# Reading a bias table back in four parts through another DMA queue, and a reworked attention stage: one core of a Trainium2 chip

## The chip, the core and the metric

One Trainium2 chip, one of its cores. The metric is the time of one execution of the program in microseconds (us). TensorE (PE) multiplies matrices and transposes, VectorE (DVE) and ScalarE (ACT) work on elements, GpSimd (POOL) does small things, and SyncE (SP) issues most of the DMAs. Each engine runs its instructions in the order in which the program hands them over; what orders the engines among themselves are semaphores.

## What is computed

A trunk of two layers on 256 tokens of width 1024, in float32. Layer 0 mixes with a state-space mixer (S5); layer 1 with sparse attention whose keys and values are computed once, between the layers.

```python
for layer in range(DEPTH):
    h = h + 0.5 * _swiglu(_rmsnorm(h, ffn1_norm[layer]), ffn1_w_in[layer], ffn1_w_out[layer])
    u = _rmsnorm(h, mix_norm[layer])
    if layer < N_A_LAYERS:
        h = h + _s5_mixer(u, ...)
    else:
        h = h + _nsa_mixer(u, kv, w_qg[b], q_norm[b], w_o[b], rel_bias)
    h = h + 0.5 * _swiglu(_rmsnorm(h, ffn2_norm[layer]), ffn2_w_in[layer], ffn2_w_out[layer])
    if layer == N_A_LAYERS - 1:
        kv = _shared_kv(h, ...)
```

In the attention, the queries of 16 heads of 64 (4 heads share one of 4 key groups) are normalised per head. Each head has three branches (compressed, selected and window keys), each a softmax over query times key plus a bias that depends on the distance of the two positions, `rel_bias[_rel_bucket(dist)]`. A gate per head and branch, the sigmoid of further columns of the query product, weighs the branches; the sum goes through `w_o`. With 256 tokens all causal blocks are selected and the window holds all tokens, so selected and window keys are both 128 columns for the first 128 tokens and 256 for the second.

## The kernel before

**Matmuls.** Tokens stand in two tiles of 128, t = 0 and 1. Every float32 product is made of three products of rounded parts (`mm3`, L126 to L128): the activations' rounding (hi) times the weights' hi, hi times the weights' remainder (lo), and lo times hi. So each weight is split on chip after loading: a granule of 1 MB lands in one of two `raw` buffers (`load_granule`, SP's queue), ACT rounds it (`whi`; L92 plain, L105 times a norm's gain), and DVE makes the remainder (`wlo`; L96, L108). There are five buffers of each. `Acts` holds a stage's transposed activations: `turn` transposes (PE), `place` writes their hi (ACT) and lo (DVE), `fill` does both for four column groups of a tile.

**Stages, in order.** First FFN of layer 0, to about 205 us; the S5 mixer to about 268; second FFN of layer 0 to about 460; the shared keys and values to about 505; first FFN of layer 1 to 700.5; attention to 808.5; second FFN of layer 1 to the end. Outside S5 and attention a scheduler at build time sets each engine's order, from the order of the program and its own estimates of when data arrives.

**An FFN** runs over 11 chunks of 256 hidden columns. A chunk takes eight `w_in` slices, 48 matmuls of 512 columns into two PSUM banks `mm`. ACT and DVE make the gated activation g (L306, L307). PE transposes the g of the chunk before (L265) in the middle of the products, ACT and DVE copy it out (`turned`, L151, L152), and 24 matmuls with `w_out` add to the result.

**The bias table.** While the second FFN of layer 0 runs, the generator `bias_tables` is stepped in its gaps (`background`, one step per two of a chunk's eight slices, paced by what each `yield` returns). It makes one row `rev` of biases per head, writes it to DRAM scratch `revd` (two DMAs), and reads it back as `KV.B`, 128 rows by 16 heads by 256 distances, each row shifted by one against the next, in eight DMAs of 256 KB on SP's queue (L846). SP's queue also carries the granules. `B` is read first in the attention.

**Attention** is an order written by hand: `ORDER` is a string of steps, and each step is issued on its engines in that order, which the scheduler keeps for PE, ACT and DVE. The letters that matter here: d, h, w load and split a part of the query weights; f, F, J fill the activations of tile 1; Q, R its norm; g the query product, four parts per group n and tile t into one `mm` bank; a to x the normalisation of its heads and the transposes (a squares and copies out of the bank on ACT, b the mean on DVE and the power -1/2 on POOL, n multiplies, i and j split, y transposes, x copies out); l the logits of one head into a bank `s` (and `x` for t = 1); v adds bias and takes the maximum (DVE), e the exponential and its sum (ACT), s and S scale the probabilities by 1/sum and gate (DVE); t transposes them and T copies them to SBUF; c, k, q, z, C, K, Z are the compressed branch; P is the product with the values, o and O copy it out; D, H, W load and split `w_o`, and M is the product with it; the last letters prepare the next FFN.

PSUM has two banks each of `mm`, `tr` (transposes), `s` and `x`. A bank is handed out again in turn, and the first matmul into it waits until all readers of its last contents are done.

## Time and profile before

| | |
|---|---|
| median of three runs | 998.76 us (998.57 to 1000.18) |
| the profiled execution, in all | 1000.22 us |
| its span, first to last instruction | 998.5 us |
| granted TensorE clock, mean over the span | 1.00 |
| PE busy | 969.4 us, 97% |
| DVE, ACT, POOL busy | 659.0, 577.1, 80.6 us |

Every row below comes from the one profiled execution. The engine that is nearly full is PE; what a stage can lose or give back is where PE waits. PE's busy time overlaps from one matmul to the next, so waits also show as fewer matmuls in a stretch of equal length.

### The profile page before, as it was taken

The numbers are of one execution on the slowest core, as the hardware profiler recorded it, in microseconds if no ns is written. First come the engines' busy times: TensorE is split into PE (matmuls) and PEld (weight loads), VectorE is DVE, ScalarE is ACT, GpSimd is POOL, SyncE is SP. The second block draws the span as 40 slices with busy tenths as digits, with TensorE's granted clock in tenths as the row PEclk, the third lists the DMA queues.
The fourth block names the chain that finished last, engine by engine and source line by source line (L and its number), as shares of the span: only waits on it lengthen the run. The fifth ranks groups of instructions, "written<-read, shape, count | busy, mean of one in ns | idle before, by whom it ended". The sixth has DMA issues, their size and how long they took to land.

```text
span 998.5 us, 14337 instructions
## 1 busy us (share of the span) xinstructions
PE 969.4 (97%) x5523; PEld 794.1 (80%) x5523; DVE 659.0 (66%) x1210; ACT 577.1 (58%) x1023; POOL 80.6 (8%) x91
## 2 busy tenths in 40 slices
PE   6999999999999989999999999999988999999998
PEld 5788788788878867788878888888876778888886
DVE  4998875579964544657566556565899676555553
ACT  5677666463663543656656545454888565555552
POOL 3001012312200000000032000000200000000000
PEclk9999999999999999999999999999999999999999
DMA  7555565433357556564644445554431235555551
GB/s 270 192 192 202 174 208 177 164 94 146 97 190 212 158 174 216 185 228 151 248 169 166 170 171 197 182 189 135 127 107 43 85 127 211 193 186 185 195 179 74
DMA packets 28948, 168.96 MB, mean 169 GB/s; under 512 B 4560, under 2 KB 7184, under 8 KB 10064
## 3 DMA queue, kind: packets, MB, share of 16 engines
q1 hardware_dynamic: 28656, 167.26, 49.7%
q8 instruction: 43, 0.70, 0.3%
q0 software_dynamic: 224, 0.79, 0.2%
q14 instruction: 25, 0.20, 0.1%
HBM read 165.54 MB, written 2.49 MB: 168 GB/s over the span
## 4 chain that ended last, share of the span: by engine, by line
PE 78%; DVE 11%; ACT 5%; DMA 4%; issue 1%; POOL 1%; SPq 0%; ACTq 0%
PE mm L126 15%; PE mm L127 15%; PE mm L128 14%; PE o L128 7%; PE o L127 7%; PE o L126 7%; DMA raw<-in_w_in_dram 3%; DVE wlo L96 3%; PE tr L265 2%; ACT whi L92 1%; DVE Pt L1153 1%; PE dr L596 1%; PE tr L945 1%; PE ga L126 1%; PE ga L128 1%
## 5 line engine op out<-in xcount | busy, mean ns | idle before, releaser
L126 PE MATMUL mm<-whi,xT 128*128 128x512 f32 (+2 forms) x800 | 312.4, 392 | 6.1 <-ACT whi L92 2.6
L127 PE MATMUL mm<-wlo,xT 128*128 128x512 f32 (+2 forms) x800 | 306.3, 383 | 0.7 <-DVE wlo L96 0.5
L128 PE MATMUL mm<-whi,xT 128*128 128x512 f32 (+2 forms) x800 | 305.9, 383 | 0.0
L108 DVE SCALAR_TENSOR_TENSOR wlo<-raw,gains,whi 128x512 fp32r<-128x512 f32 x274 | 192.7, 748 | 86.7 <-ACT whi L105 84.1
L105 ACT ACTIVATE whi<-raw,gains 128x512 fp32r<-128x512 f32 x274 | 182.6, 718 | 98.8 <-PE mm L128 50.1
L96 DVE TENSOR_TENSOR wlo<-raw,whi 128x1024 fp32r<-128x1024 f32 x132 | 160.5, 1224 | 104.4 <-ACT whi L92 103.8
L92 ACT ACTIVATE whi<-raw 128x1024 fp32r<-128x1024 f32 x132 | 138.4, 1059 | 121.5 <-PE mm L128 51.5
L126 PEld LDWEIGHTS mm<-whi,xT 128*128 128x128 f32 x800 | 150.7, 189 | 37.1 <-ACT whi L105 3.1
L127 PEld LDWEIGHTS mm<-wlo,xT 128*128 128x128 f32 x800 | 151.1, 189 | 29.4 <-DVE wlo L96 1.5
L128 PEld LDWEIGHTS mm<-whi,xT 128*128 128x128 f32 x800 | 150.7, 188 | 29.3
L128 PE MATMUL o<-whi,turned 128*128 128x512 f32 x352 | 137.5, 391 | 0.8 <-DVE turned L152 0.8
L127 PE MATMUL o<-wlo,turned 128*128 128x512 f32 x352 | 137.6, 391 | 0.1
L126 PE MATMUL o<-whi,turned 128*128 128x512 f32 x352 | 136.8, 391 | 0.0
L128 PEld LDWEIGHTS o<-whi,turned 128*128 128x128 f32 x352 | 66.1, 188 | 15.0 <-DVE turned L152 1.5
L127 PEld LDWEIGHTS o<-wlo,turned 128*128 128x128 f32 x352 | 66.1, 188 | 14.4 <-DVE wlo L96 1.0
L126 PEld LDWEIGHTS o<-whi,turned 128*128 128x128 f32 x352 | 66.0, 188 | 13.7
L306 ACT ACTIVATE g<-mm,rs 128x256 f32<-128x256 f32 x88 | 41.0, 472 | 45.2 <-PE mm L128 44.9
L307 DVE SCALAR_TENSOR_TENSOR g<-mm,rs,g 128x256 f32<-128x256 f32 x88 | 41.7, 482 | 36.2 <-ACT g L306 36.1
L152 DVE TENSOR_TENSOR turned<-tr,turned 128x512 fp32r<-128x512 f32 x44 | 30.3, 688 | 36.1 <-ACT turned L151 35.7
L151 ACT ACTIVATE turned<-tr 128x512 fp32r<-128x512 f32 x44 | 26.1, 593 | 45.9 <-PE tr L265 45.9
L148 POOL TENSOR_TENSOR rs<-ms,nhalf 128x1 f32<-128x1 f32 x12 | 7.6, 633 | 284.4 <-DVE ms L147 284.4
L1160 ACT ACTIVATE Pt<-Pt,mx 128x128 f32<-128x128 f32 (+1 forms) x64 | 28.3, 446 | 3.7 <-DVE mx L1153 3.7
(321 smaller groups left out, 982.0 us busy)
## 6 DMA issues: line engine op xcount, KB each, us to landing
raw<-in_w_in_dram SPq DMA_DIRECT2D x87, 1024.0 KB, 4.9
raw<-in_w_out_dram SPq DMA_DIRECT2D x44, 1024.0 KB, 4.9
raw<-in_w_kv_dram SPq DMA_DIRECT2D x6, 1024.0 KB, 4.8
raw<-in_w_glu_dram SPq DMA_DIRECT2D x4, 1024.0 KB, 4.9
raw<-in_w_o_dram SPq DMA_DIRECT2D x4, 1024.0 KB, 5.0
raw<-in_w_qg_dram SPq DMA_DIRECT2D x6, 512.0 KB, 3.6
B<-revd SPq DMA_DIRECT2D x8, 256.0 KB, 7.5
raw<-in_w_qg_dram SPq DMA_DIRECT2D x2, 608.0 KB, 3.8
```

The source lines that it names most:

```text
L92: Last.act = S.activation(hi, r, AF.Copy)
L96: Last.dve = V.tensor_tensor(out=lo, in0=r, in1=hi.bitcast(F32), op=ALU.subtract)
L105: Last.act = S.activation(hi[:, c], r[:, c], AF.Identity, scale=g_)
L108: i = V.scalar_tensor_tensor(out=lo[:, c], in0=r[:, c], scalar=g_, in1=hi[:, c].bitcast(F32), op0=ALU.mult, op1=ALU.subtract)
L126: T.matmul(ps, lhsT=xh, rhs=wh, start=start, stop=False)
L127: T.matmul(ps, lhsT=xh, rhs=wl, start=False, stop=False)
L128: Last.pe = T.matmul(ps, lhsT=xl, rhs=wh, start=False, stop=stop_)
L151: i = S.activation(dst_hi, src, AF.Copy)
L152: V.tensor_tensor(out=dst_lo, in0=src, in1=dst_hi.bitcast(F32), op=ALU.subtract)
L306: Last.act = S.activation(sl, acc[t][:, 0:256], AF.Silu, scale=rs[:, t:t + 1])
L307: Last.dve = V.scalar_tensor_tensor(out=g[:, t, :], in0=acc[t][:, 256:512], scalar=rs[:, t:t + 1], in1=sl, op0=ALU.mult, op1=ALU.mult)
L1160: S.activation(p_, p_, AF.Exp, scale=-1.0, bias=mx[g, t][:, c:c + 1], accum_out=sm[g, t][:, c:c + 1])
```

## The change

**Bias table.** The host lays `rel_bias` out so that 32 rows of `rev` hold four heads, eight times. `revd` becomes four scratch tensors of four heads. For each of them two DMAs on SP's queue write it from 32 rows of `rev`, and eight DMAs on GpSimd's queue, of 64 KB, read it back into `B` (L845 after): 32 reads in place of 8, of the same bytes in all. Every read is followed by a `yield` of one step.

**Fill with a gain** (`Acts.fill`): the roundings of all four column groups (ACT) are issued ahead of the four remainders (DVE), where the two alternated.

**Attention.** Step a only squares, unscaled; the scaled copy `qs` is gone (eight ACT instructions, L1094), step n reads the bank itself, and step b takes the row's mean in place of a constant so that the missing scale cancels. The gate's tanh is a step of its own (p). Key columns of tile 0's logits stand in another order, so that one matmul of 272 columns takes what 400 took (32 matmuls, L1138). The multiplication by `vcol` is done once in G in place of once per group in k. Step s is the reciprocal alone, and S multiplies by both the reciprocal and the gate (64 instructions, L1205). Of the 24 copies of transposed probabilities, 21 (T) are on ACT and 3 (X) on DVE, where each had 12. `ORDER` is a new list, of 399 steps for 397. The diff shows one line of it, before and after; new names of the same lines and some unchanged lines are left out.

```diff
@@ -142,8 +142,8 @@
...
-    def row_rstd(t, ss, rs):
-        ms = small.tile([P, 1], F32, name="ms")
+    def row_rstd(t, ss, rs, ms=None):
+        ms = small.tile([P, 1], F32, name="ms") if ms is None else ms[:, t:t + 1]
         V.scalar_tensor_tensor(out=ms, in0=ss[:, 2 * t:2 * t + 1], scalar=EPS, in1=ss[:, 2 * t + 1:2 * t + 2], op0=ALU.add, op1=ALU.add)
         G.tensor_tensor(out=rs[:, t:t + 1], in0=ms, in1=nhalf[:, 0:1], op=ALU.pow)
@@ -159,6 +159,7 @@
...
+            self.ms = small.tile([P, 2], F32, name="mean")
@@ -192,8 +193,7 @@
...
             else:
-                for j in range(4):
-                    i = [self.place(u, t, kq, pv, (j,)) for u in range(2)][0]
+                i = [self.place(u, t, kq, pv) for u in range(2)][0]
@@ -835,16 +835,15 @@
...
         yield
-        dr = dscr.tile([16, 16, 384], F32, name="revd")
-        for r in range(2):
-            nc.sync.dma_start(out=dr[8 * r:8 * r + 8].rearrange("q h k -> (q h) k"), in_=rev)
-            yield
-        yield
         KV.B = kp.tile([P, 16, 256], F32, name="B")
-        for r in range(8):
-            src = bass.AP(tensor=dr.tensor, offset=dr.offset + 127 - 16 * r, ap=[[16 * 384 - 1, 16], [384, 16], [1, 256]])
-            nc.sync.dma_start(out=KV.B[16 * r:16 * r + 16], in_=src)
-            yield 4
+        for n in range(4):
+            dr = dscr.tile([16, 4, 384], F32, name=f"revd{n}")
+            for q in range(2):
+                nc.sync.dma_start(out=dr[8 * q:8 * q + 8].rearrange("q h k -> (q h) k"), in_=rev[32 * n:32 * n + 32])
+            for r in range(8):
+                src = bass.AP(tensor=dr.tensor, offset=dr.offset + 127 - 16 * r, ap=[[4 * 384 - 1, 16], [384, 4], [1, 256]])
+                nc.gpsimd.dma_start(out=KV.B[16 * r:16 * r + 16, 4 * n:4 * n + 4], in_=src)
+                yield
@@ -934,7 +933,7 @@
...
-                    c0 = (n - 1) * KWN + t * P
+                    c0 = (1 - t) * P if n == 1 else KWN + t * P
@@ -995,21 +994,21 @@
...
-    Q0 f0 d10 g000 F00 f1 g001 J00 d11 F01 h100 F10 J01 w100 d20 F11 g010 J10 g002 h110 J11 Q1 g011 g003 g012 R g013 a00 w110 b00
...
+    d10 g000 Q0 d11 h100 f0 w100 g001 f1 g002 F00 F01 d20 J01 g003 F11 J00 Q1 J11 g010 g011 a00 R F10 b00 J10 h110 p0 g012 w110
...
@@ -1074,7 +1073,7 @@
...
             def step_R():
-                row_rstd(1, x.ss, rs)
+                row_rstd(1, x.ss, rs, x.ms)
@@ -1086,30 +1085,28 @@
...
             def step_a(n, t):
-                q, v = tp.tile([P, 256], F32, name="qs"), tp.tile([P, 4, 2, 64], F32R, name="qst")
-                qq[n, t], qv[n, t] = q, v
-                if n == 0:
-                    S.activation(rsh[:, t:t + 1], rs[:, t:t + 1], AF.Copy, scale=0.5)
-                S.activation(v.rearrange("p h a d -> p (h a d)")[:, 0:256].bitcast(F32), qa[n, t][:, 0:256], AF.Square, scale=rs[:, t:t + 1])
-                S.activation(q, qa[n, t][:, 0:256], AF.Identity, scale=rs[:, t:t + 1])
-                if n == 0:
-                    S.activation(gate[:, t].rearrange("p h b -> p (h b)"), qa[n, t][:, 256:304], AF.Tanh, scale=rsh[:, t:t + 1])
+                qq[n, t], qv[n, t] = tp.tile([P, 256], F32, name="qs"), tp.tile([P, 4, 2, 64], F32R, name="qst")
+                S.activation(qv[n, t].rearrange("p h a d -> p (h a d)")[:, 0:256].bitcast(F32), qa[n, t][:, 0:256], AF.Square)
+
+            def step_p(t):
+                S.activation(rsh[:, t:t + 1], rs[:, t:t + 1], AF.Copy, scale=0.5)
+                S.activation(gate[:, t].rearrange("p h b -> p (h b)"), qa[0, t][:, 256:304], AF.Tanh, scale=rsh[:, t:t + 1])
...
             def step_b(n, t):
-                ss, ms = tp.tile([P, 4], F32, name="hss"), tp.tile([P, 4], F32, name="hms")
+                ss, ms = (tp.tile([P, 4], F32, name=u, bufs=4) for u in ("hss", "hms"))
                 sq = qv[n, t].rearrange("p h a d -> p (h a d)")[:, 0:256].bitcast(F32)
                 V.tensor_reduce(out=ss, in_=sq.rearrange("p (h d) -> p h d", d=64), axis=mybir.AxisListType.X, op=ALU.add)
-                V.tensor_scalar(out=ms, in0=ss, scalar1=1.0, scalar2=64 * EPS, op0=ALU.mult, op1=ALU.add)
-                rr = tp.tile([P, 4], F32, name="hrr")
+                V.scalar_tensor_tensor(out=ms, in0=x.ms[:, t:t + 1].to_broadcast([P, 4]), scalar=64 * EPS, in1=ss, op0=ALU.mult, op1=ALU.add)
+                rr = tp.tile([P, 4], F32, name="hrr", bufs=4)
                 G.tensor_tensor(out=rr, in0=ms, in1=nhalf[:, 0:4], op=ALU.pow)
                 qp[n, t] = rr
 
             def step_n(n, t):
-                q3 = qq[n, t].rearrange("p (h d) -> p h d", d=64)
-                V.tensor_tensor(out=q3, in0=q3, in1=qp[n, t].unsqueeze(2).to_broadcast([P, 4, 64]), op=ALU.mult)
+                q3, a3 = (u[:, 0:256].rearrange("p (h d) -> p h d", d=64) for u in (qq[n, t], qa[n, t]))
+                V.tensor_tensor(out=q3, in0=a3, in1=qp[n, t].unsqueeze(2).to_broadcast([P, 4, 64]), op=ALU.mult)
@@ -1129,30 +1126,32 @@
...
             def step_G():
                 V.tensor_scalar(out=gate, in0=gate, scalar1=0.5, scalar2=0.5, op0=ALU.mult, op1=ALU.add)
+                V.tensor_scalar(out=gate[:, 0, :, 0], in0=gate[:, 0, :, 0], scalar1=vcol, scalar2=None, op0=ALU.mult)
             def step_l(g, t, r):
                 ps = s_bank()
-                parts = [(ps[:, 0:400], 0, 400)] if t == 0 else [(ps[:, 0:KWN], 0, KWN), (x_bank()[:, 0:256], KWN, KW)]
+                parts = [(ps[:, 0:KWN], P, P + KWN)] if t == 0 else [(ps[:, 0:KWN], 0, KWN), (x_bank()[:, 0:256], KWN, KW)]
...
-                lb[g, t, r] = ps, ps[:, KWN:400] if t == 0 else parts[1][0]
+                lb[g, t, r] = (ps[:, 0:P], ps[:, P:KC], ps[:, KWN - P:KWN]) if t == 0 else (ps[:, 0:KC], ps[:, KC:KWN], parts[1][0])
             def step_v(g, t, r):
...
-                    mx[g, t], sm[g, t] = tp.tile([P, 8], F32, name="mx"), tp.tile([P, 8], F32, name="sm", bufs=4)
+                    mx[g, t], sm[g, t] = tp.tile([P, 8], F32, name="mx", bufs=4), tp.tile([P, 8], F32, name="sm", bufs=4)
...
-                ps, win = lb[g, t, r]
+                sel, cmp_, win = lb[g, t, r]
                 for br in range(2):
                     c = r * 2 + br
-                    V.tensor_tensor_reduce(out=Pt[g, t][:, r, br], in0=win if br else ps[:, 0:nk], in1=KV.B[:, hh, 256 - nk:256],
+                    x_, b_, o_ = (u.rearrange("p (k c) -> p k c", c=P) for u in (win if br else sel, KV.B[:, hh, 256 - nk:256], Pt[g, t][:, r, br]))
+                    V.tensor_tensor_reduce(out=o_, in0=x_ if br else x_[:, ::-1], in1=b_,
                                            scale=-1.0, scalar=3e38, op0=ALU.add, op1=ALU.min, accum_out=mx[g, t][:, c:c + 1])
-                V.tensor_tensor(out=cl[g][:, t, r, 0:nv], in0=ps[:, KC:KC + nv], in1=KV.B[:, hh, k0:k0 + 16 * (nv - 1) + 1:16], op=ALU.add)
+                V.tensor_tensor(out=cl[g][:, t, r, 0:nv], in0=cmp_[:, 0:nv], in1=KV.B[:, hh, k0:k0 + 16 * (nv - 1) + 1:16], op=ALU.add)
@@ -1172,7 +1171,6 @@
...
                 V.tensor_tensor(out=u, in0=u, in1=gate[:, :, g * 4:g * 4 + 4, 0], op=ALU.mult)
-                V.tensor_scalar(out=u[:, 0], in0=u[:, 0], scalar1=vcol, scalar2=None, op0=ALU.mult)
                 V.tensor_tensor(out=cl[g], in0=cl[g], in1=u.unsqueeze(3).to_broadcast([P, 2, 4, 15]), op=ALU.mult)
@@ -1194,15 +1192,13 @@
...
             def step_s(g, t):
-                u = sm[g, t]
-                V.reciprocal(u, u)
-                V.tensor_tensor(out=u.rearrange("p (r b) -> p r b", b=2), in0=u.rearrange("p (r b) -> p r b", b=2),
-                                in1=gate[:, t, g * 4:g * 4 + 4, 1:3], op=ALU.mult)
+                V.reciprocal(sm[g, t], sm[g, t])
             def step_S(g, t, br):
                 for r in range(4):
                     c = r * 2 + br
-                    V.tensor_scalar(out=Pt[g, t][:, r, br], in0=Pt[g, t][:, r, br], scalar1=sm[g, t][:, c:c + 1], scalar2=None, op0=ALU.mult)
+                    V.tensor_scalar(out=Pt[g, t][:, r, br], in0=Pt[g, t][:, r, br], scalar1=sm[g, t][:, c:c + 1],
+                                    scalar2=gate[:, t, g * 4 + r, br + 1:br + 2], op0=ALU.mult, op1=ALU.mult)
@@ -1210,13 +1206,16 @@
...
-            def step_T(g, t, kb, br):
-                pts[g, t, kb, br] = pt_room[:, turn[0] % 4]
+            def pt_next(*u):
+                pts[u] = pt_room[:, turn[0] % 4]
                 turn[0] += 1
-                if br:
-                    V.tensor_copy(pts[g, t, kb, br], tp_[g, t, kb, br])
-                else:
-                    S.activation(pts[g, t, kb, br], tp_[g, t, kb, br], AF.Copy)
+                return pts[u], tp_[u]
+
+            def step_T(*u):
+                S.activation(*pt_next(*u), AF.Copy)
+
+            def step_X(*u):
+                V.tensor_copy(*pt_next(*u))
@@ -1334,7 +1333,7 @@
...
-                    row_rstd(0, Nxt.x.ss, Nxt.x.rs)
+                    row_rstd(0, Nxt.x.ss, Nxt.x.rs, Nxt.x.ms)
@@ -1418,7 +1417,7 @@
...
-    A["rel_bias"] = np.tile(I["rel_bias"], (1, 8))
+    A["rel_bias"] = np.tile(I["rel_bias"].reshape(32, 4, 1, 4), (1, 1, 8, 1)).reshape(32, 128)
```

What the three engines then have in their queues, at three places. First ACT in the second FFN of layer 0, before from about 327 to 369 us (L105 and L92 round weights, L306 is the gate's activation, L151 copies the transposes out). Before:

```order
L306 ACTIVATE g<-mm,rs 128x256 x2
L105 ACTIVATE whi<-raw,gains 128x512 x7
L151 ACTIVATE turned<-tr 128x512
L105 ACTIVATE whi<-raw,gains 128x512
L92 ACTIVATE whi<-raw 128x1024 x2
L306 ACTIVATE g<-mm,rs 128x256 x2
L105 ACTIVATE whi<-raw,gains 128x512 x4
L151 ACTIVATE turned<-tr 128x512
L105 ACTIVATE whi<-raw,gains 128x512 x4
L92 ACTIVATE whi<-raw 128x1024 x2
L306 ACTIVATE g<-mm,rs 128x256 x2
L151 ACTIVATE turned<-tr 128x512
```

and now:

```order
L151 ACTIVATE turned<-tr 128x512
L105 ACTIVATE whi<-raw,gains 128x512 x2
L306 ACTIVATE g<-mm,rs 128x256 x2
L105 ACTIVATE whi<-raw,gains 128x512 x4
L92 ACTIVATE whi<-raw 128x1024 x2
L105 ACTIVATE whi<-raw,gains 128x512 x2
L151 ACTIVATE turned<-tr 128x512
L105 ACTIVATE whi<-raw,gains 128x512 x2
L306 ACTIVATE g<-mm,rs 128x256 x2
L105 ACTIVATE whi<-raw,gains 128x512 x4
```

Now a chunk's rows come in the same order from chunk to chunk, with two L105 on either side of L151. Before, L151 stood behind four L105 or seven, with two or four of the next behind it, or directly behind L306.

Second, PE where the FFN (`o`) ends and attention begins (L167, now L168, transposes tile 1 for the fill; `mm` is the first query product), before:

```order
L126 MATMUL o_4524<-whi,turned 128x512
L127 MATMUL o_4524<-wlo,turned 128x512
L128 MATMUL o_4524<-whi,turned 128x512
L167 MATMUL tr<-ident,h 128x128 x4
L126 MATMUL mm<-whi,xT 128x304
L127 MATMUL mm<-wlo,xT 128x304
```

and now:

```order
L127 MATMUL o_4560<-wlo,turned 128x512
L128 MATMUL o_4560<-whi,turned 128x512
L126 MATMUL mm<-whi,xT 128x304
L127 MATMUL mm<-wlo,xT 128x304
L128 MATMUL mm<-whi,xT 128x304
L126 MATMUL mm<-whi,xT 128x304
L127 MATMUL mm<-wlo,xT 128x304
L128 MATMUL mm<-whi,xT 128x304
L168 MATMUL tr<-ident,h 128x128 x4
L126 MATMUL mm<-whi,xT 128x304
```

The four transposes have moved behind the six matmuls of the first part of the query product.

Third, DVE at the first normalisation of queries (L1104 and L1101 sum the squares, L1112 and L1109 multiply by the power that POOL makes between, L1118 and L1115 make the remainder, L1062 and L1061 split weights), before:

```order
L1104 TENSOR_REDUCE hss<-qst 128x4
L1105 TENSOR_SCALAR hms<-hss 128x4
L1104 TENSOR_REDUCE hss<-qst 128x4
L1105 TENSOR_SCALAR hms<-hss 128x4
L1112 TENSOR_TENSOR qs<-qs,hrr 128x256
L1062 TENSOR_TENSOR wlo<-raw,whi 128x1024
L1118 TENSOR_TENSOR qst<-qs,qst 128x4x64
L1112 TENSOR_TENSOR qs<-qs,hrr 128x256
L1062 TENSOR_TENSOR wlo<-raw,whi 128x1024
L1118 TENSOR_TENSOR qst<-qs,qst 128x4x64
```

and now:

```order
L1101 TENSOR_REDUCE hss<-qst 128x4
L1102 SCALAR_TENSOR_TENSOR hms<-mean,hss 128x4
L179 SCALAR_TENSOR_TENSOR xT<-tr,gains,xT 128x128 x2
L1061 TENSOR_TENSOR wlo<-raw,whi 128x1024
L1109 TENSOR_TENSOR qs<-mm,hrr 128x256
L1115 TENSOR_TENSOR qst<-qs,qst 128x4x64
L1101 TENSOR_REDUCE hss<-qst 128x4
L1102 SCALAR_TENSOR_TENSOR hms<-mean,hss 128x4
L1061 TENSOR_TENSOR wlo<-raw,whi 128x1024
L1128 TENSOR_SCALAR gate<-gate 128x96
L1129 TENSOR_SCALAR gate<-gate,vcol 128x16
```

The multiplication now reads the bank `mm` itself, so the bank is held until it is done; the gate's multiplication by `vcol` stands here once.

## Rows read from the trace of the kernel before

**Rows 1.** Page, part 1: engine, busy us (share of span) and instructions, PE's line.

```profile
PE 969.4 (97%) x5523; PEld 794.1 (80%) x5523; DVE 659.0 (66%) x1210; ACT 577.1 (58%) x1023; POOL 80.6 (8%) x91
```

**Rows 2.** Windows, second FFN of layer 0: us, then PE, PEld, DVE, ACT, POOL, clock.

```profile
350.00:375.00 25.00, 22.30 (x99) 17.40 (x98) 12.51 (x19) 11.40 (x18) 0.00 (x0) 1.00 0.56 166
375.00:400.00 25.00, 24.18 (x107) 19.21 (x106) 10.19 (x15) 8.48 (x14) 0.00 (x0) 1.00 0.70 220
400.00:425.00 25.00, 24.18 (x107) 19.19 (x106) 17.48 (x25) 16.12 (x25) 0.00 (x0) 1.00 0.58 182
425.00:450.00 25.00, 25.00 (x116) 20.69 (x115) 14.42 (x18) 12.49 (x18) 0.00 (x0) 1.00 0.67 237
```

**Rows 3.** PE's waits, 290 to 460 us: us in total, times, longest.

```profile
PE mm L126 <- ACT whi L105: 2.6, 2, 1.3
PE tr L265 <- DVE g L307: 1.5, 4, 0.4
```

**Rows 4.** Timeline of ACT: start, us, instruction, [idle before it and its releaser].

```profile
347.19 2.57 ACT L105 ACTIVATE whi<-raw,gains 128x512 fp32r<-128x512 f32 x4 [2.09 <-DMA raw<-in_w_in_dram]
355.95 0.60 ACT L151 ACTIVATE turned<-tr 128x512 fp32r<-128x512 f32 x1 [6.19 <-PE tr L265]
356.44 2.56 ACT L105 ACTIVATE whi<-raw,gains 128x512 fp32r<-128x512 f32 x4
```

**Rows 5.** Timeline of PE beside it.

```profile
357.21 0.73 PE L126 MATMUL mm<-whi,xT 128*128 128x512 f32 x2 [1.30 <-ACT whi L105]
```

**Rows 6.** Tile B: its eight reads on SP (issue time in ns) and their landing.

```profile
L846 SPq DMA_DIRECT2D B<-revd x8: 383/425/441, 305.2 to 395.7; - x8
...
DMA to landing us min/median/max: 7.3/7.5/9.1
```

**Rows 7.** A DMA issued by POOL: issue time in ns.

```profile
L435 POOL DMA_DIRECT2D WBT<-in_s_b_dram x1: 741/741/741, 7.6 to 7.6; - x1
```

**Rows 8.** Windows, attention: columns as in rows 2.

```profile
700.50:784.00 83.50, 75.22 (x509) 63.06 (x508) 77.23 (x332) 69.89 (x218) 10.30 (x11) 1.00 0.29 93
784.00:808.50 24.50, 24.50 (x153) 17.98 (x152) 14.67 (x35) 12.01 (x25) 0.56 (x1) 1.00 0.18 56
```

**Rows 9.** PE's waits, 700.5 to 784 us: the first two.

```profile
PE s L1138 <- DVE clg L1155: 2.8, 5, 1.3
PE tr L167 <- DVE xT L178: 1.5, 1, 1.5
```

**Rows 10.** Groups by form, 690 to 810 us: instruction, count | busy us, mean ns.

```profile
L1205 DVE TENSOR_SCALAR Pt<-Pt,sm 128x256 f32<-128x256 f32 x32 | 9.1, 346 | 0.0
...
L1107 POOL TENSOR_TENSOR hrr<-hms,nhalf 128x4 f32<-128x4 f32 x8 | 8.4, 1049 | 28.4 <-DVE hms L1105 28.3
L1217 DVE COPY turned<-tr 128x512 f32<-128x512 f32 x12 | 8.2, 684 | 3.9 <-PE tr L1210 3.9
...
L1219 ACT ACTIVATE turned<-tr 128x512 f32<-128x512 f32 x12 | 7.0, 592 | 4.2 <-PE tr L1210 4.2
L1205 DVE TENSOR_SCALAR Pt<-Pt,sm 128x128 f32<-128x128 f32 x32 | 6.9, 279 | 0.0
...
L1094 ACT ACTIVATE qs<-mm,rs 128x256 f32<-128x256 f32 x8 | 3.7, 468 | 0.0
...
L1112 DVE TENSOR_TENSOR qs<-qs,hrr 128x256 f32<-128x256 f32 x8 | 3.3, 416 | 0.0
...
L1199 DVE TENSOR_TENSOR sm<-sm,gate 128x8 f32<-128x8 f32 x8 | 1.3, 167 | 0.3
```

**Rows 11.** Source L344, a scaling by two constants: ns min, median, max.

```profile
L344 DVE TENSOR_SCALAR sinT<-sinT x4: 420/426/1614, 52.2 to 95.9; 128x512 f32<-128x512 f32 x4
```

**Rows 12.** Source L699, a scaling by one column of pointers.

```profile
L699 DVE TENSOR_SCALAR xT<-h,rs x1: 489/489/489, 209.9 to 209.9; 128x512 f32<-128x512 f32 x1
```

**Rows 13.** Timeline of PE at the start of the program.

```profile
9.58 0.79 PE L126 MATMUL mm<-whi,xT 128*128 128x512 f32 x1 [2.60 <-ACT whi L92]
```

**Rows 14.** Timeline of ACT at the start.

```profile
6.95 0.62 ACT L180 ACTIVATE xT<-tr,gains 128x128 fp32r<-128x128 f32 x2 [0.42 <-DVE xT L178]
```

More of the change, by code (lines that the diff above doesn't have):

```diff
@@ L1006 @@
-    e201 P100 W10 e202 i31 e203 j31 O01 W11 t1100 T1100 o10 y21 t1110 O10 s20 x21 a30 T1110 H20 t1111 b30 l210 T1111 v210 P110 e210
-    P111 S201 l211 y31 W20 o11 x31 O11 v211 n30 l212 l310 e211 i30 v212 v310 l311 l312 j30 t2001 e310 v311 S200 e311 l313 y30 v312
-    T2001 e212 x30 v313 D3 l213 t2000 l300 v213 M00 l301 e213 e312 T2000 v300 l302 c2 e300 e313 s21 S211 v301 e301 M01 S210 v302
-    l303 C2 t2100 t2101 s31 k2 v303 H21 K2 T2101 H30 T2100 M10 e302 q2 W21 c3 z2 C3 M11 W30 k3 Z2 e303 P200 s30 S311 t2111 T2111
@@ L1010 @@
-    t2110 H31 K3 T2110 o20 q3 S301 P210 O20 S300 z3 Z3 P211 t3001 t3000 S310 L0 W31 M20 T3001 T3000 o21 t3101 P300 t3100 T3101 o30
-    t3110 O30 T3110 T3100 O21 M30 N0 t3111 A01 P310 B01 T3111 A00 V0 P311 B00 Y00 o31 O31 L1 M21 M31 Y01 N1 N2 U01 U00 V1 A10 B10
-    A11 B11 Y11 Y10 U11 U10 V2
+    d10 g000 Q0 d11 h100 f0 w100 g001 f1 g002 F00 F01 d20 J01 g003 F11 J00 Q1 J11 g010 g011 a00 R F10 b00 J10 h110 p0 g012 w110
+    d21 n00 g013 h200 g110 i00 a01 j00 y00 g111 p1 b01 w200 x00 l000 G v000 E l001 d30 g112 l002 h210 n01 i01 v001 v002 g113 a11
@@ new lines @@
+    j01 e000 g100 b11 y01 x01 l003 e001 g101 h300 l010 w210 g102 e002 v003 e003 l011 g103 v010 n11 a10 i11 w300 g210 v011 l012
+    g211 e010 b10 j11 v012 s00 l013 g212 e011 e012 v013 y11 x11 d31 e013 n10 c0 g213 S001 g200 l110 S000 a21 i10 t0001 l111 v110
+    b21 t0000 g201 v111 T0001 j10 C0 h310 l112 g202 T0000 e110 e111 y10 l113 w310 k0 v112 x10 K0 g203 l100 D0 a20 n21 v113 b20
+    i21 H00 g300 j21 l101 g301 y21 e112 v100 g302 H01 g303 x21 q0 s01 W00 l102 n20 z0 W01 v101 g310 e100 i20 e113 S010 D1 Z0 a30
@@ new lines @@
+    l103 j20 v102 v103 S011 y20 t0100 g311 b30 e101 x20 c1 T0100 e102 t0110 l200 H10 v200 t0111 P000 l201 C1 s11 e200 e103 g312
+    g313 W10 T0110 T0111 k1 t0101 s10 l202 K1 n30 v201 a31 T0101 S110 S100 v202 l203 P010 e201 H11 i30 t1000 q1 T1000 o00 b31 D2
+    P011 S101 v203 j30 z1 O00 H20 t1001 o01 Z1 n31 O01 l210 y30 T1001 W11 S111 e202 i31 x30 t1100 T1100 P100 v210 j31 t1111 o10
+    O10 T1111 l300 v300 t1101 l211 W20 T1101 e203 t1110 T1110 v211 l301 P110 e210 y31 P111 s20 v301 x31 l310 o11 S200 S201 O11
@@ new lines @@
+    v310 t2000 l311 v311 T2000 e300 l212 l312 e310 v212 v312 l313 v313 l213 v213 c2 t2001 l302 v302 e311 e312 e211 e212 X2001 C2
+    k2 e213 K2 M00 e313 e301 l303 v303 s21 M01 q2 S211 c3 t2101 C3 H21 k3 T2101 M10 D3 z2 e302 W21 M11 K3 H30 s31 Z2 e303 S210
+    s30 W30 t2100 P200 S301 H31 t2110 T2100 T2110 o20 S311 q3 t2111 S300 P210 T2111 t3001 z3 P211 S310 T3001 t3100 Z3 O20 o21
+    W31 X3100 t3000 M20 T3000 t3101 T3101 L0 O21 N0 t3111 M21 P300 o30 t3110 V0 P310 O30 T3110 X3111 N1 M30 A01 P311 A00 B01 B00
@@ L1013 @@
+    o31 O31 Y01 V1 Y00 L1 U01 U00 M31 N2 A10 B10 A11 V2 Y10 B11 Y11 U10 U11
     """
```

7 lines of the change are left out of this document (removed).

## The prediction

> **What bounds the kernel now.** I read the page's first part, then the windows of the stages that the change touches, then PE's waits there, then the timelines at the longest waits. PE is busy 97% of the span [rows 1], so nearly all the time is PE work; an edit pays where PE waits or where it takes PE work away. The change touches three places. In the second FFN of layer 0, a full window of 25 us holds 116 matmuls, and three windows in a row hold 99, 107 and 107 [rows 2]: PE waits there. In attention up to 784 us PE is busy 75.2 of 83.5 us, DVE 77.2, ACT 69.9; from there to 808.5 PE is full [rows 8]. At the start of the program PE waits 2.6 us for the first rounded weights [rows 13].
>
> What stops PE in the FFN is an order, not a slow transfer. The timelines show it: ACT rounds four slices, then sits 6.19 us until PE has done the transposes, copies them out at 355.95, and rounds the next four slices from 356.44 without a wait for their data [rows 4]. PE needs the first of those four and stands 1.30 us [rows 5]. The slices had landed; they stood behind a copy that waits for PE. All the waits named are 4.1 us [rows 3]; but matmuls after a wait come further apart too (two in 0.73 us, where a full window has one per 25/116 = 0.216 us [rows 5, 2]). So I count matmuls: 17 + 9 + 9 = 35 missing, times 0.216, is 7.5 us lost.
>
> **Bias table.** Before, eight reads of 256 KB go out on SP's queue between 305.2 and 395.7 us and land 7.3 to 9.1 us later [rows 6]; the three poor windows lie in and right behind that stretch. The scheduler at build time placed ACT's copies by its own idea of when the granules come, with these reads in the same queue. In the new order of ACT, shown above, the irregular rows are gone: two rounded slices stand on each side of the copy in every chunk, one chunk like the next. So I take back the 7.5 us. What is late next there: nothing on ACT, whose 16.1 us in the fullest of these windows leave 9 free [rows 2]. The reads themselves: 32 on POOL at 0.74 us of issue [rows 7] are 24 us on an engine that has no work in these windows [rows 2], so they hide; who would wait is `B`'s first reader, some 300 us later. Eight writes for two on SP's queue are six more issues of 0.43 us [rows 6], 2.6 us over a stage of 190 us, in front of granules. If both irregular places stayed, 0 comes back (the first rival); if one of two stays, half, 3.75. The most is 7.5.
>
> **Fill with a gain.** At the start ACT waits 0.42 us between roundings, for DVE's remainder of the column before [rows 14]; now it only waits for PE. The weights' rounding stands behind these on ACT, and PE waits 2.6 us for it [rows 13]. Against it, DVE starts its remainders no earlier, and PE has four more transposes to do before the first product. I take one such wait, 0.5 us; the ends are 2.5 (all of PE's wait) and -1.0 (two of them, 0.42 each, lost again on DVE's side). The fill at the end of the FFN of layer 1 hides behind 512-column products.
>
> **Attention, work by engine.** DVE: nine copies of 0.684 go to ACT (6.16), eight gate products of 0.167 are gone (1.34), four small products by `vcol` become one (three of 0.167, 0.50; rows 10 have no row of their own for them, L1199 is the nearest): -8.0. The second pointer of S is in no row. From below it costs 0: one pointer on 256 elements takes 346 ns, on 128 it takes 279, 0.52 ns per element and 212 fixed [rows 10], so the rate is one thing and the operands another. From above it costs what the first pointer does, 489 against 426 ns with two constants [rows 11, 12], 0.063 on 64 instructions, 4.0 us. I take 0, since with two constants [rows 11] the second operand is there already and the rate is no lower than with one pointer, and keep 4.0 for the rival. ACT: eight copies of 0.468 gone (3.74), nine of 0.592 more (5.33): +1.6. PE: 32 matmuls of 272 columns for 400, 128 columns each at 0.216/4 = 0.054: -1.7. So after, in the stretch to 784: DVE 77.2 - 8.0 = 69.2, ACT 71.5, PE 73.5.
>
> The tier table of the page "VectorE: DVE Perf Modes" of the Trainium skill (§ The perf-mode tier table) gives float32 `tensor_scalar` from SBUF a doubled rate and makes no difference by where its scalars come from; no run here has two pointers, and by the page the second one would cost nothing, by the upper bound of rows 4.0 us on DVE.
>
> **Attention, what it is worth.** Today the busiest engine, DVE, leaves 83.5 - 77.2 = 6.3 us of the stretch unfilled. If the new order leaves as much on its busiest engine, PE, the stretch is 73.5 + 6.3 = 79.8: 3.7 us gained. Besides, 1.5 us that PE waited for the fill at the very start [rows 9] goes, as the transposes now stand behind the first product's six matmuls (the order above). That is 5.2; I take 5. The rest is one-for-one: step b's other instruction costs what it did, step n reads PSUM at the same price (its old form, 0.416 [rows 10], is a two-tensor product too), the reversed read of the bias is a change of addresses. The most is all of PE's idle time and its columns, 8.3 + 1.7 = 10; the least in my own case is 1, when the unfilled time on PE rises from 6.3 to 9. The stretch behind 784 is full of PE work and stays.
>
> **A wait is added:** a bank `mm` is now held until step n has read it, where ACT's two copies freed it. The eight query products share two banks, so six products reuse one. Extra: sum 0.42 (taken as n's price), mean 0.17, power 1.05 on POOL, n 0.42, less the copy 0.47 [rows 10]: 1.6 us, plus what stands ahead on DVE. Behind the waiting matmul, all of PE's queue stands. In the new list logits and transposes worth 3 to 6 us of PE time stand between the last read-out and the reuse, so I cost it at nothing.
>
> **Sum.** 7.5 + 5 + 0.5 = 13.0. The profiled execution took 1000.22 us in all, with a span of 998.5; it would take 987.2. The median is 998.76, 1.46 less, so 985.8.
>
> **Rivals.**
> First, the table's cost stays: the reads move the same bytes, granules come late just as before, and the new regular order meets slices that have not landed. For it: ACT waited 2.09 us for a granule's landing at 347 [rows 4]. Against it: that wait was covered, and the stall came later. Then only 5.5 us come: 998.76 - 5.5 = 993.3. Chance 0.12.
>
> The page "DMA: Bandwidth & Descriptors" of the Trainium skill (§ Issuing engines are not separate DMA queues) speaks for it: transfers issued by SP, ACT or POOL end on the same 16 engines and interleave, so that several issuers save issue time only. No row here shows both issuers at once.
>
> Second, attention gives nothing. With the second pointer at 4.0 us DVE stands at 73.2, ACT at 71.5, PE at 73.5: three engines evenly filled, each waiting for the others in a list in which no one can run ahead, and the unfilled time on the busiest grows from 6.3 to 10. Against it: PE's longest named wait there, 2.8 us for v's reading of the logits [rows 9], is for DVE, whose load falls most. 998.76 - 8.0 = 990.8. Chance 0.17.
>
> Third, slower: the bank. If at each of six reuses two S steps (4 x 0.346 each [rows 10], 2.8) stand ahead of b or n on DVE, a reuse costs 1.6 + 2.8 = 4.4 us; with no cover on PE that is 26 us, less 13.0: 998.76 + 13 = 1012. It decides from 13.0/6 = 2.2 us of uncovered wait per reuse. Against it: the 3 to 6 us of other work. Chance 0.06.
>
> **How the numbers follow.** 0.2%, about 2 us, is what a measurement of this kernel can tell from no change. Forecast 0.61 (985.8), rivals 0.12, 0.17, 0.06, and 0.04 that gains and losses meet within 0.2%. The range: low end 998.76 - (7.5 + 10 + 2.5) = 979; high end with half the table's gain, the least of attention and the loss at the start, 998.76 - (3.75 + 1 - 1) = 995. It holds the first two rivals; left out are the third, the middle case and the forecast's tails. Faster by over 0.2%: 0.61 + 0.12 + 0.17 = 0.90. Within: 0.04. Slower: 0.06.
>
> **What would show it.** Table: the windows from 350 to 425 us hold 115 or so matmuls each, and PE waits for no L105 there; `B`'s reads are POOL's. If PE waits instead for ACT and ACT for raw data, the first rival is right. Attention: DVE near 69 us and the S rows at 346 and 279 ns (0.06 more: the second pointer costs); the logits' 32 matmuls at 272 columns; PE's idle time in the stretch near 6. The bank: waits of the query products (`mm`, lines of `mm3`) on DVE's step n; over 2 us each, the third rival is right. The start: PE's first product before 9.6 us. I am wrong as a whole if the windows after 350 are full and the time is still above 995.

## The result, and the profile after

The changed kernel takes 984.37 us (983.20 to 984.86, four runs) against 998.66 us before: a ratio of 0.9853, 95% interval 0.9841 to 0.9865. The forecast was 985.8 with a range of 979 to 995. The profiled execution took 984.86 us, 15.4 less than that of before.

PE's timeline gives the length of each stage (the FFNs by their first and last matmul into `o`; attention from the last such matmul to the first product of the next FFN):

| stage | before | after | gained | forecast |
|---|---|---|---|---|
| start to the end of the first FFN | 206.7 us | 203.5 | 3.2 | 0.5 |
| second FFN of layer 0 | 172.1 | 165.0 | 7.1 | 7.5 |
| attention | 108.3 | 102.7 | 5.6 | 5 |
| all others | the same within 0.3 | | -0.3 | 0 |

The total came out near the forecast in part by luck: the start gave six times its forecast, and in attention terms that were wrong both ways cancelled. The page's first part answers [rows 1]; PE is busy for 7.6 us less:

```profile
PE 961.8 (98%) x5523; PEld 793.3 (81%) x5523; DVE 656.1 (67%) x1190; ACT 580.9 (59%) x1024; POOL 98.4 (10%) x123
```

The windows of the second FFN answer [rows 2] (us, then PE, PEld, DVE, ACT, POOL, clock):

```profile
350.00:375.00 25.00, 25.00 (x116) 20.67 (x115) 14.54 (x20) 13.44 (x20) 4.05 (x8) 1.00 0.65 202
375.00:400.00 25.00, 25.00 (x114) 20.69 (x113) 14.76 (x20) 13.05 (x19) 0.00 (x0) 1.00 0.59 193
400.00:425.00 25.00, 25.00 (x116) 20.67 (x115) 14.49 (x19) 13.38 (x20) 0.00 (x0) 1.00 0.54 186
```

They hold 114 to 116 matmuls where they held 99 to 107, and the list of PE's waits from 285 to 460 us is empty. The tile `B` [rows 6] is now read by POOL, 0.51 us of issue each and not 0.74:

```profile
L845 POOL DMA_DIRECT2D B<-revd x32: 514/514/587, 301.0 to 367.3; - x32
...
DMA to landing us min/median/max: 2.4/5.0/7.1
```

In attention the windows answer [rows 8], cut so that the full last stretch of 24.5 us is the same work:

```profile
690.50:768.50 78.00, 71.98 (x507) 61.92 (x506) 72.34 (x310) 68.56 (x214) 10.85 (x11) 1.00 0.31 101
768.50:793.00 24.50, 24.50 (x153) 17.85 (x152) 14.16 (x33) 11.97 (x24) 0.00 (x0) 1.00 0.16 48
```

The stretch is 78.0 us for 83.5. DVE is still its busiest engine, 72.3 us, and leaves 5.7 unfilled where it left 6.3. PE's waits there [rows 9]: us in total, times, longest.

```profile
PE s L1136 <- DVE clg L1154: 2.0, 5, 1.0
PE tr L1121 <- DVE qst L1115: 1.9, 3, 1.1
PE mm L126 <- DVE qs L1109: 1.0, 1, 1.0
PE x L1136 <- DVE oT L1243: 0.8, 2, 0.6
```

All four are waits for DVE. The groups by form answer [rows 10] (count | busy us, mean ns | idle before):

```profile
L1215 ACT ACTIVATE turned<-tr 128x512 f32<-128x512 f32 x21 | 12.4, 594 | 6.8 <-PE tr L1206 6.3
...
L1200 DVE TENSOR_SCALAR Pt<-Pt,sm,gate 128x256 f32<-128x256 f32 x32 | 11.0, 405 | 0.0
L1104 POOL TENSOR_TENSOR hrr<-hms,nhalf 128x4 f32<-128x4 f32 x8 | 10.1, 1260 | 28.1 <-DVE hms L1102 28.0
...
L1200 DVE TENSOR_SCALAR Pt<-Pt,sm,gate 128x128 f32<-128x128 f32 x32 | 8.7, 343 | 0.0
```

The scalings S rose from 346 and 279 ns to 405 and 343: the second pointer costs 0.06 us each, 3.9 us in all.

At the start, PE's timeline answers [rows 13] (start, us, instruction, [idle before it]):

```profile
10.20 1.09 PE L168 MATMUL tr<-ident,h 128*128 128x128 f32 x4 [2.75 <-DMA h<-in_x_dram]
10.94 1.60 PE L126 MATMUL mm<-whi,xT 128*128 128x512 f32 x2
...
13.62 0.61 PE L128 MATMUL mm<-whi,xT 128*128 128x512 f32 x1
14.04 0.42 PE L126 MATMUL mm<-whi,xT 128*128 128x512 f32 x1
14.30 0.40 PE L127 MATMUL mm<-wlo,xT 128*128 128x512 f32 x1
```

Here, after the transposes of the third group, PE waits for nothing more, and its matmuls take 0.40 us from 14.3 on. The prediction's sign for the start, PE's first product before 9.6 us, did not come: it starts at 10.94, later than the 9.58 of before.

### The profile page after: what moved, and what is told of

The parts are those of the page before. It is cut to its first block, busy times and chain, and to the rows that moved or that the text cites. A ratio compares the mean times of both kernels' runs of the same rounds, so it can differ in the third digit from the quotient of the medians.

```text
span 982.9 us, 14385 instructions
## 1 busy us (share of the span) xinstructions
PE 961.8 (98%) x5523; PEld 793.3 (81%) x5523; DVE 656.1 (67%) x1190; ACT 580.9 (59%) x1024; POOL 98.4 (10%) x123
## 4 chain that ended last, share of the span: by engine, by line
PE 90%; DVE 6%; ACT 1%; DMA 1%; issue 0%; POOL 0%; SPq 0%; DVEq 0%; ACTq 0%
PE mm L126 17%; PE mm L128 17%; PE mm L127 17%; PE o L126 8%; PE o L127 8%; PE o L128 8%; PE tr L265 2%; DVE Pt L1152 1%; PE dr L596 1%; DVE Pt L1200 1%; PE tr L944 1%; PE ga L126 1%; PE ga L128 1%; DMA h<-in_x_dram 1%; PE ga L127 1%; PE tr L168 1%
## 5 line engine op out<-in xcount | busy, mean ns | idle before, releaser
L105 ACT ACTIVATE whi<-raw,gains 128x512 fp32r<-128x512 f32 x274 | 184.1, 719 | 108.5 <-PE mm L128 65.3
L92 ACT ACTIVATE whi<-raw 128x1024 fp32r<-128x1024 f32 x132 | 139.1, 1061 | 139.3 <-PE mm L128 60.5
L306 ACT ACTIVATE g<-mm,rs 128x256 f32<-128x256 f32 x88 | 41.2, 473 | 33.9 <-PE mm L128 33.6
L151 ACT ACTIVATE turned<-tr 128x512 fp32r<-128x512 f32 x44 | 26.1, 594 | 20.7 <-PE tr L265 20.7
L265 PE MATMUL tr<-ident,g 128*128 128x128 f32 x176 | 26.6, 272 | 0.0
```

Of the source, the lines that this page charges most:

```text
L92: Last.act = S.activation(hi, r, AF.Copy)
L105: Last.act = S.activation(hi[:, c], r[:, c], AF.Identity, scale=g_)
L265: T.transpose(ps[:, (f * 2 + t) * P:(f * 2 + t + 1) * P], g[:, t, f * P:(f + 1) * P], ident)
L306: Last.act = S.activation(sl, acc[t][:, 0:256], AF.Silu, scale=rs[:, t:t + 1])
```

## The experiments

All are timed in five rounds beside the kernel before. "After" is the changed kernel, 984.37 us.

**Bias table alone**, in the kernel before (the diff of `bias_tables` and `rel_bias` above, nothing else).

> The kernel before with the bias table's change alone (four parts on GpSimd's queue, rel_bias laid out for them). Theory: the table's reads on SP's queue made the build-time scheduler order ACT irregularly in the second FFN of layer 0, and the waits of PE there, 7.1 us between the two traces, go with this part alone: 991.5 us, full windows of 115 matmuls from 350 to 425 us. Rival: the gain in that stretch needs the other edits too, or is shared with them: 995 or more.

991.65 us (990.81 to 993.62), 0.9921 of before (0.9907 to 0.9936), 7.0 us gained. The second FFN takes 164.7 us, and its windows are full. The part stands alone, as the theory said. The profiled execution is the slowest of the five, 993.62 us, with attention at 110.2 us for 108.3; the granted clock there fell to 0.86 and 0.80 between 755 and 765 us, which the profile of before does not show.

**Fill alone**, in the kernel before (the diff of `fill`).

> The kernel before with the fill's order alone (four roundings, then four remainders). Theory: the start of the program gains 3.2 us by it, as the first transposes of the g stand 3.4 us earlier in the trace of after: 995.5 us. Rival, the size of the prediction: 0.5 us, and the rest of the start's gain is chance in the first loads: 998.2 us.

996.07 us (995.11 to 996.62), 0.9967 (0.9954 to 0.9980): 2.6 us. The size of the prediction, 0.5, falls. The first FFN ends at 202.5 us; over the twelve kernels with this fill it ended between 202.0 and 205.0, 203.1 in the mean, without it at 205.7 (the table alone) and 206.7, so a single profile gives this term to a microsecond and a half or so. Attention, with the old list, gets 0.6 us shorter too (107.7): PE's wait for the fill there [rows 9] is gone, and 1.1 us of waits for the gate's tanh have come:

```profile
PE mm L126 <- ACT gate L1095: 1.1, 2, 0.8
```

No run has the attention's edits alone. What table (7.0) and fill (2.6) leave of the 14.3 us between the medians is 4.7.

**The 32 small reads on SP.**

```diff
-                nc.gpsimd.dma_start(out=KV.B[16 * r:16 * r + 16, 4 * n:4 * n + 4], in_=src)
+                nc.sync.dma_start(out=KV.B[16 * r:16 * r + 16, 4 * n:4 * n + 4], in_=src)
```

> The changed kernel with the 32 reads of 64 KB issued by SP in place of GpSimd. Theory: what counts is the queue, as the order at build time follows from reads that share a queue with the granules; ACT's order is irregular again and PE waits as before: 984.4 + 7 = 991.5 us. Rival: what counts is the smaller size of the reads: 984.4 us.

989.23 us (988.27 to 990.26), 4.9 more than after. In ACT's order L151 stands again behind four, six or eight L105, or behind none, and the stage takes 170.8 us. Its windows, then PE's waits from 285 to 460 us:

```profile
325.00:350.00 25.00, 24.44 (x108) 19.41 (x107) 13.42 (x19) 11.51 (x19) 0.00 (x0) 1.00 0.63 197
350.00:375.00 25.00, 24.18 (x107) 19.17 (x107) 12.75 (x18) 11.50 (x18) 0.00 (x0) 1.00 0.59 193
375.00:400.00 25.00, 23.88 (x102) 18.16 (x101) 12.86 (x18) 12.14 (x19) 0.00 (x0) 1.00 0.52 176
```

```profile
PE tr L265 <- DVE g L307: 2.0, 5, 0.4
```

Small reads on SP do not help much; with the reads in the granules' queue the order is irregular. It is so on PE as well: some transposes of g stand directly behind the last product that makes this g, and PE waits for it, where in the changed kernel 24 matmuls with `w_out` and 30 products of the next chunk stand between. Late granules are not what PE's named waits are for: ACT waits 29.0 us in all for granules from 285 to 465 us (20.9 before, 8.2 after), but none of PE's waits is for a rounding.

**Eight large reads on GpSimd**, against the kernel before:

```diff
-            nc.sync.dma_start(out=KV.B[16 * r:16 * r + 16], in_=src)
+            nc.gpsimd.dma_start(out=KV.B[16 * r:16 * r + 16], in_=src)
```

(with the two writes, `revd` and `rel_bias` of before, in the changed kernel)

> The changed kernel with the bias table read back as before in eight reads of 256 KB, but on GpSimd's queue (rel_bias and the two writes as before). Theory: the queue alone decides; ACT's order is regular, PE waits nowhere in the second FFN of layer 0: 984.4 us. Rival: large reads in front of granules delay them on the engines: 2 to 7 us slower.

995.38 us (993.37 to 996.62), 11.0 slower than after; the stage takes 174.4 us. The theory that the queue alone decides falls. ACT's order is the same as after, but once the writes have landed nothing holds POOL back: the eight reads go out within 4 us and take 14.4 us to land in the median and 24.4 at most; the granules behind them are late. Tile `B`, then ACT's timeline, then PE's:

```profile
L846 POOL DMA_DIRECT2D B<-revd x8: 563/563/646, 301.9 to 305.9; - x8
...
DMA to landing us min/median/max: 7.4/14.4/24.4
```

```profile
325.03 2.00 ACT L92 ACTIVATE whi<-raw 128x1024 fp32r<-128x1024 f32 x2 [13.24 <-DMA raw<-in_w_out_dram]
330.22 1.33 ACT L105 ACTIVATE whi<-raw,gains 128x512 fp32r<-128x512 f32 x2 [3.19 <-DMA raw<-in_w_in_dram]
331.46 0.57 ACT L151 ACTIVATE turned<-tr 128x512 fp32r<-128x512 f32 x1
```

```profile
332.09 0.80 PE L126 MATMUL o<-whi,turned 128*128 128x512 f32 x1 [7.59 <-ACT turned L151]
```

ACT waits 13.2 and 3.2 us for granules, and the copy of the transposes, which needs no granule, stands behind them; PE stands still for 7.6 us. The page "DMA: Bandwidth & Descriptors" of the Trainium skill (§ Issuing engines are not separate DMA queues) says that transfers of all issuers interleave on the same 16 engines; this trace agrees: the engines are busy without a gap (DMA share, the column before the last, 0.98 to 1.08 from 304 to 328 us), and the two `w_out` granules issued from 300 to 340 us landed after 11.3 us in the median, where 4.9 is usual.

**Every small read twice**, on GpSimd.

```diff
-                nc.gpsimd.dma_start(out=KV.B[16 * r:16 * r + 16, 4 * n:4 * n + 4], in_=src)
+                for _ in range(2):
+                    nc.gpsimd.dma_start(out=KV.B[16 * r:16 * r + 16, 4 * n:4 * n + 4], in_=src)
```

> The changed kernel with each of the 32 reads of the bias table done twice on GpSimd's queue (the same bytes to the same place), so that the transfers there double from 2 MB to 4 MB while ACT's order stays regular. Theory: transfers beside the granules cost nothing, only the order did: 984.4 us, windows full. Rival: the 16 engines are shared and granules come late: 2 to 7 us slower, waits of ACT for raw data in the windows from 300 to 400 us.

984.69 us (983.21 to 985.77): the same as after, with twice the bytes. The reads spread over 81 us:

```profile
L846 POOL DMA_DIRECT2D B<-revd x64: 512/514/587, 302.7 to 383.4; - x64
```

So bytes beside the granules are free as long as they come a little at a time. These were paced too: POOL stood 37.5 us in three waits for a part's writes and 37.3 us in thirteen for an earlier read into the same place (in the changed kernel 76.7 us in four waits for writes). Taken with the two before: the queue sets the order at build time, and the parts, each of which waits for its own writes on SP's queue, keep the reads from crowding the granules. The change needs both, another queue and the parts; whether the parts act by the pacing or by the smaller reads was not separated.

**One pointer in S**: s and S as before the change, the gate's product on DVE.

> The changed kernel with the steps s and S of before: the product with the gate in s (8 DVE instructions of 0.167 us), one pointer in S. After, S took 405 and 343 ns where before it took 346 and 279, so 64 second pointers cost 3.9 us of DVE; undone, DVE has 2.6 us less work in attention. Theory: DVE still sets most of PE's waits there, and 1 to 2.6 us come back: 981.8 to 983.4 us. Rival: the second pointer lies beside other engines' work: 984.4 us.

982.45 us (981.89 to 983.49), 0.9835 of before (0.9820 to 0.9850), 1.9 less than after; attention takes 100.9 us, 1.8 less. The lines of S are back:

```profile
L1203 DVE TENSOR_SCALAR Pt<-Pt,sm 128x256 f32<-128x256 f32 x32 | 9.1, 346 | 0.0
L1203 DVE TENSOR_SCALAR Pt<-Pt,sm 128x128 f32<-128x128 f32 x32 | 6.8, 282 | 0.0
```

Of 2.6 us less on DVE by these rows (2.1 in its busy time), 1.8 reach the end. This is the lowest median of the study, but its runs touch those of after (981.89 to 983.49 and 983.20 to 984.86), and so do the intervals of the two ratios. The stage says more: the attention of after took 101.8 to 102.7 us in the four kernels that leave it alone, so 0.9 to 1.8 us are gained there.

**The gate's product on GpSimd**, with one pointer in S.

```diff
...
+                u3 = sm[g, t].rearrange("p (r b) -> p r b", b=2)
+                G.tensor_tensor(out=u3, in0=u3, in1=gate[:, t, g * 4:g * 4 + 4, 1:3], op=ALU.mult)
...
```

> The changed kernel with one pointer in S and the product with the gate in s on GpSimd, which has little to do in attention. DVE has 3.9 us less work, and each of 8 chains from s to S gets a GpSimd instruction of about 1 us (its powers on 128x4 take 1.0 to 1.3 us). Theory (DVE's load sets PE's waits): 1 to 3.9 us faster, 980.5 to 983.4 us, and at least as fast as with the product on DVE. Rival: the longer chain to S is waited for: 984.4 us or more.

982.84 us (981.87 to 983.33): 1.5 less than after, attention 100.4 us. The product took 0.53 us on POOL in the mean; DVE waited for it 0.2 us in all. It cannot be told from the kernel with the product on DVE.

**Copies in halves**: of the 24 copies of probabilities, ten T become X and one X becomes T (12 on each engine), at the same places of the list.

> The changed kernel with the copies of transposed probabilities split as before: 12 on DVE and 12 on ACT, at the same places of the list (nine copies of 0.69 us move from ACT to DVE). Theory: DVE's load sets PE's waits in attention; 2.6 us of DVE work less gave 1.6 us of the stage, so 6.2 us more cost 3 to 4: 987.4 to 988.5 us. Rival: the gain came from the new list, whichever engine copies: 984.4 us, or less as ACT has 5.3 us less.

988.21 us (987.82 to 989.26): 3.8 slower than after, attention 106.1 us, in the theory's range. Its windows, to hold against those of after:

```profile
690.50:772.00 81.50, 73.38 (x513) 62.23 (x513) 77.15 (x320) 65.98 (x207) 10.83 (x11) 1.00 0.29 97
```

DVE has 77.2 us again, as before the change, and the stretch is 81.5. The move of nine copies is 3.4 us of attention's 5.6. At this same load of DVE the stretch before was 83.5: 2.0 us come from the rest of the edits, the fill and the list among them, and no run separates those.

**The bank freed early.**

```diff
+                S.activation(qq[n, t], qa[n, t][:, 0:256], AF.Copy)
...
-                q3, a3 = (u[:, 0:256].rearrange("p (h d) -> p h d", d=64) for u in (qq[n, t], qa[n, t]))
+                q3, a3 = (u[:, 0:256].rearrange("p (h d) -> p h d", d=64) for u in (qq[n, t], qq[n, t]))
```

> The changed kernel with a copy of the query product out of its bank on ACT in step a (8 instructions of about 0.47 us, as before the change), and step n reading that copy, so that the bank is free after ACT. Theory: the held bank costs one named wait, 1.0 us at 698 us, and ACT's 3.7 us of added work cost about as much: 984 to 986 us, with the wait of mm on step n gone. Rival (the prediction's third rival in small): the held bank costs more than the trace names, 2 us or more come back: below 982.5 us.

984.15 us (983.90 to 984.47): no change. The wait on the bank is gone from PE's list, and the next one for the same chain is longer by nearly as much (after: 1.9):

```profile
PE tr L1122 <- DVE qst L1116: 2.7, 2, 1.5
PE s L1137 <- DVE clg L1155: 2.0, 5, 1.0
```

What PE waits for is the chain of the first normalisation; through the bank or through the transposes makes no difference, and eight copies on ACT, 3.1 us, cost nothing.

**400 key columns** for the first tile.

```diff
-                parts = [(ps[:, 0:KWN], P, P + KWN)] if t == 0 else ...
+                parts = [(ps[:, 0:400], 0, 400)] if t == 0 else ...
```

> The changed kernel with the logits of the first tile computed over 400 key columns again, in the new order of columns (32 matmuls, 128 columns each more, 1.7 us of PE). Theory: PE's work is on the path nearly everywhere in attention, so 1.0 to 1.7 us are lost: 985.4 to 986.1 us. Rival: PE waits for DVE there anyway and the columns fill its waits: 984.4 us.

984.57 us (983.28 to 985.05): no change that the runs can tell. A loss of 1 us could hide in the medians; the stage decides against the theory. Attention takes 102.5 us for 102.7, while PE is busy 73.2 us in the stretch for 72.0 and the waits have shrunk (after: 2.0 and 1.9):

```profile
PE s L1136 <- DVE clg L1154: 1.4, 3, 1.0
PE tr L1121 <- DVE qst L1115: 1.2, 2, 1.0
```

**The list's old first steps**: Q0 and f0 alone stand in front again.

```diff
-    d10 g000 Q0 d11 h100 f0 w100 g001 ...
+    Q0 f0 d10 g000 d11 h100 w100 g001 ...
```

> The changed kernel with the first steps of the list as before: the square and the first transposes of tile 1 ahead of the query product. Theory of the prediction: PE waits for the fill of tile 0 there as before, 1.5 us, so 985.9 us. Rival: the new order of the fill (roundings first, remainders ready sooner) has already taken that wait away, since with the fill's edit alone the transposes no longer waited: 984.4 us.

983.64 us (983.55 to 984.49): no slower. The prediction's theory falls; no wait of the transposes for the fill is in the list. The fill's edit had removed it.

**Half of w_o's remainders on GpSimd**, on top of the gate's product there.

```diff
...
+                if j < 2:
+                    G.tensor_tensor(out=wl["o", j, i], in0=r_, in1=h_, op=ALU.subtract)
...
```

> The kernel with the gate's product on GpSimd, and besides the remainders of half of w_o's weights (4 of 8, 128x1024) on GpSimd in place of DVE. DVE has 4.8 us less work again. Theory (DVE's load sets PE's waits, about 0.6 us of the stage for each us): 2 to 3 us faster than the 982.8 with the gate's product alone, 980 to 981 us. Rival: GpSimd's instructions of two us or more stand ahead of its powers of the head means, or slow DVE's steps beside them: 982.8 us or more.

987.85 us (987.35 to 988.75): 5.0 slower than with the gate's product alone, attention 106.8 us. The rival is right. POOL's timeline, then DVE's:

```profile
725.65 2.37 POOL L1257 TENSOR_TENSOR wlo<-raw,whi 128x1024 fp32r<-128x1024 f32 x1
```

```profile
726.33 2.63 DVE L1202 TENSOR_SCALAR Pt<-Pt,sm 128x256 f32<-128x256 f32 x4
...
730.20 1.13 DVE L1202 TENSOR_SCALAR Pt<-Pt,sm 128x256 f32<-128x256 f32 x4
```

Four scalings that take 1.13 us at 730 take 2.63 beside POOL's subtraction, which ends at 728.0. The work that was taken from DVE still held it. The other half of the rival is there too: a power of the head means stands behind a subtraction on POOL (724.41 us), and DVE waits 0.79 us for it. And the granted clock of TensorE (column after POOL) fell in this stage, where that of after stays at 1.00:

```profile
728.00:732.00 4.00, 2.57 (x18) 2.60 (x19) 3.96 (x22) 2.83 (x12) 0.02 (x2) 0.84 0.74 246
732.00:736.00 4.00, 4.00 (x25) 3.02 (x24) 3.39 (x11) 3.69 (x12) 3.30 (x3) 0.74 0.05 20
740.00:750.00 10.00, 8.26 (x52) 6.23 (x49) 7.71 (x30) 6.46 (x16) 3.48 (x3) 0.83 0.31 105
```

How much of the 5.0 us is the clock's was not separated. It is not most of it: the mean clock of the profiled execution, 988.75 us, is 0.997, and another with 0.999 still took 987.45.

## Why the prediction was right, point by point

**Table: right in size (7.5, measured 7.1), right in its mechanism, incomplete in its reason.** The step "an order, not a slow transfer" holds: small reads on SP bring the irregular order and 5.8 us of the stage back, and doubled bytes on POOL cost nothing. But I read the order on ACT alone. PE's is part of it: before, four waits of 1.5 us in all are of transposes for g [rows 3], and with the small reads on SP these are the only ones named. I also costed the reads at nothing because POOL is idle, and took the four parts for a detail. Eight reads on the same idle POOL cost 9.4 us in that stage. The first rival, late granules, was weighed by a row that could not decide it; its mechanism is real, and the parts keep it off. Four parts whose reads do not wait for their own writes were not tried.

**Fill: the step that failed.** I took one wait of 0.42 us [rows 14] and gave 2.5 as the most; 3.2 came between the profiles, 2.6 by the kernel with that edit alone, of which 0.6 may lie in attention. The path failed: I had the weights' rounding, and with it PE's first product, come earlier, and both came later (8.80 us for 8.47, 10.94 for 9.58): `h` landed 0.5 us later, and the first product now stands behind transposes that wait 2.75 us for more of `h`. The mis-sized term is what follows at this place. Before, ACT waited for DVE's remainder again, 1.04 us ahead of 11.08, and PE for a weight's remainder, 0.47 us ahead of 10.84. Its matmuls were still slow at 15.25 us and reached 0.40 us at 16.37; the timeline of before:

```profile
12.72 0.63 PE L128 MATMUL mm<-whi,xT 128*128 128x512 f32 x1
...
15.25 1.05 PE L127 MATMUL mm<-wlo,xT 128*128 128x512 f32 x2
16.37 0.40 PE L126 MATMUL mm<-whi,xT 128*128 128x512 f32 x1
```

After, the step to 0.40 us comes at 14.3 us all the same: some 2 us more at full pace. The wait of PE for DVE's g at 26.0 us is gone as well. That matmuls run on slowly after a wait was in rows I had used for the FFN, and I did not use it here. How the gain divides between slow matmuls and waits was not tried.

**Attention: right in sum (5; measured 5.6 in the profiles, 4.7 left by the medians), by terms that were wrong both ways.** The columns' 1.7 us of PE, the wait of 1.5 us by the new first steps, and the free second pointer all failed. The columns only fill waits for DVE. The wait went by the fill, and another for the gate's tanh came with it under the old list. The pointer costs what its upper bound said, 3.9 us of DVE, of which the end sees 1.8; that the rate per element stays (0.48 ns between 343 and 405, 0.52 before) was true and no argument, as the price is a fixed 0.06 us an instruction. What carried most of the stage is the step "what the busiest engine leaves unfilled": DVE left 6.3 us before, 5.7 after, 4.4 with copies in halves (81.5 - 77.15), while its work went from 77.2 to 72.3 and back. I had put PE in as the busiest engine after, by the free pointer; it is DVE, at 72.3, with PE at 72.0. The tier table of the page "VectorE: DVE Perf Modes" of the Trainium skill (§ The perf-mode tier table) has one entry for float32 `tensor_scalar` from SBUF, wherever its scalars come from; the measured 0.06 us decides.

**The added wait: right.** One reuse of a bank is waited for, 1.0 us, where six at 4.4 us were the rival; and without the bank's hold the time is the same.

**Second rival** (attention gives nothing): its price for the pointer was right and its conclusion wrong; DVE at 72.3 beside PE at 72.0 did not widen the unfilled time.

## What to carry to other kernels

A DMA that shares a queue with a kernel's stream can cost through the order that a build-time scheduler derives from it, without PE waiting for any transfer: compare the engines' orders chunk by chunk before blaming bandwidth. Moving it to an idle queue takes away the pacing as well, so something has to keep it from crowding the stream; here the four parts did. And where one engine's work sets a stage, as DVE's did here, judge every edit by that engine's sum, second operands included: PE work saved under its waits was worth nothing.
